# A decoder trunk's last gate: finished token block by token block, with the residual's scratch writes on ScalarE's queue

## The chip, the cores and the metric

The kernel runs on one core of one Trainium2 chip, as one launch. The metric is device time in microseconds (us), the median of repeated executions. The profile is a separate execution, taken by the hardware profiler; its time is given beside the others. TensorE (PE) does the matmuls, VectorE (DVE) and ScalarE (ACT) the elementwise work, GpSimd (POOL) some of it, and SyncE (SP) issues nearly all DMAs. Each engine works through its own queue in order.

## The reference, cut to what matters

A two-layer decoder trunk on 512 tokens of 1024 features, all in float32. The change is in the last two steps: the gated per-layer embedding of layer 1 and the final norm.

```python
def conv_ffn(xn, w_up, conv_w, conv_b, w_down):
    ...
    return (jax.nn.silu(g) * u) @ w_down

def per_layer_embed(h, p_i, g_norm, w_in, w_gate, b_gate):
    gate = jax.nn.sigmoid(rmsnorm(h, g_norm) @ w_gate + b_gate)
    return (p_i @ w_in) * gate

# reference(): for each layer
    h = h + conv_ffn(rmsnorm(h, norm_ffn[i]), ...)
    h = h + per_layer_embed(h, p[i], norm_ple[i], ple_w_in[i], ple_w_gate[i], ple_b_gate[i])
# at the end
    return rmsnorm(h, norm_final)
```

So the last gate needs the finished residual `h` of a token for its norm, then a 1024 x 1024 product, a sigmoid, a product with `p @ w_in`, an addition to `h`, and the mean square of the result for the final norm.

## The kernel before

**Numbers and layout.** Each float32 operand of a product is split into a high part (a cast to float32r) and a low part (the rest), and three matmuls are done for each block: high by high, low by high, high by low (`mm3`, `mm3t`). The residual lies with features on the partitions: eight tiles `h[0]` to `h[7]` of 128 features x 512 tokens. The products up to the last feed-forward keep that layout. The last gate turns it over: `mm3t` takes the normed residual as the stationary operand and the weights as the moving one, so its results have 128 tokens on the partitions and 512 features (a column half) along the row. There are four token blocks (`NC`) with two column halves each, eight feature blocks k in every product: 24 matmuls of 512 columns for a half. Because the gated result is in token layout, the old residual is needed in that layout too.

**Weights.** A planner lists all weights as units of at most 1024 columns. `load` brings a unit from HBM into one of six raw buffers (`RAWS`, tags r0 to r5), `pump_hi` lets ScalarE cast it to its high part (L187) and `pump` lets VectorE subtract for the low part (L196), into one of four pairs of buffers (`WBUFS`). The second column half of the last gate has buffers of its own: eight units of 512 columns in slots of the feed-forward's activations (`own`, `own_ah` and `own_al` in the profile). `chunk` hands a product its units and pumps a few units ahead. `load` is only called from `pump_hi` in this part of the kernel.

**The last down-projection.** `ffn(1, ...)` ends in `dense_add`: four chunks of 256 features, two blocks m each. For every block VectorE adds the product to `h[m]` (L383), then `norm.take(m)` makes the gate's scaled high and low operands (L280, L281) and the squares for its norm (L309, summed on GpSimd at L314, the last one on VectorE). Then `then(m)`, which is `turn_h(m)`: VectorE turns 32 x 32 blocks of `h[m]` into a tile `ht` (L965; tag c0, two buffers), and `write` sends the tile of the block before to a scratch array `rows` in HBM, four DMAs from SP (L959) of 64 KB each in runs of 128 bytes. The scratch array holds the residual in token layout; eight DMAs (L998) read it back into `hT`, in the order of the column halves.

**The last gate.** The first column half of all four token blocks runs with k = 0 to 5 first (72 matmuls), then k = 6 and 7 block by block; behind block 0's come eight small matmuls that sum the squares (`ms`, L990). From `ms` VectorE and GpSimd make the norm's root `np1rt` (L355, L357). Then, for each token block and half, `gated`: VectorE scales the product and adds the bias (`biased`, z, L1009), ScalarE takes the sigmoid (L1015), VectorE multiplies by the embedding and adds to `hT` (`summed`, L1016 and L1018); `square` sums the squares on ScalarE (L1028). The four first halves are gated together; then come the second halves of blocks 0 and 1, each with its final norm (`mean`, `root`, L1054), turned back (L1057) and written to `out` from SP (L1060); then block 2's second half and block 3's second half in two quarters. GpSimd multiplies the first halves of blocks 2 and 3 by the final gain ahead (L1044). Blocks 2 and 3 go out in token layout (`out_b`, L1078 and L1095).

**Order.** The framework orders the instructions of an engine by their place in the program and by when it reckons them ready, so one that is ready earlier can be moved ahead of its place. The last part (from `gate6` on) is held in the written order on VectorE, ScalarE and GpSimd by `in_order`; SP is not. SP's and ACT's DMAs signal their landing through a common set of semaphores.

Of the kernel before, what the change touches and what calls it, by code (L numbers as in the profile page):

```python
# [8 lines left out]
F32 = mybir.dt.float32  # L9
F32R = mybir.dt.float32r  # L10
U32 = mybir.dt.uint32
AF = mybir.ActivationFunctionType
ALU = mybir.AluOpType
# [39 lines left out]
def tile_yoco(ctx: ExitStack, tc: tile.TileContext, t, out: bass.AP, out_b: bass.AP):  # L53
# [12 lines left out]
    def psum(name, tag=None):  # L66
        if tag is None:
            tag = banks["tags"][banks["at"] % len(banks["tags"])]
            banks["at"] += 1
        return mmp.tile([P, S], F32, tag=tag, bufs=4 if tag == "mm" else 1, name=name)  # L70
# [135 lines left out]
    def chunk(cols, kk, ahead=WBUFS):  # L206

        pump(state["next"] + ahead)
        parts = []
        while len(parts) < kk:  # L210
            wh, wl, n = take()
            parts += [(wh, wl, j * cols) for j in range(n // cols)]
        assert len(parts) == kk
        return parts
# [11 lines left out]
    def mm3t(ps, xs, parts, c0, n, tok, first=True, last=True):  # L226

        for k, ((wh, wl, off), (xh, xl)) in enumerate(zip(parts, xs)):
            a, b = off + c0, off + c0 + n
            s = slice(tok * P, (tok + 1) * P)  # L230
            st = first and k == 0
            en = last and k == len(parts) - 1
            nc.tensor.matmul(ps, xh[:, s], wh[:, a:b], start=st, stop=False)
            nc.tensor.matmul(ps, xl[:, s], wh[:, a:b], start=False, stop=False)
            nc.tensor.matmul(ps, xh[:, s], wl[:, a:b], start=False, stop=en)
# [59 lines left out]
    class Norm:  # L295
# [11 lines left out]
        def square(self, k, eng=None):  # L307
            sq = tp.tile([P, S], F32, tag="sq", name=f"{self.name}sq{k}")
            nc.scalar.activation(sq, h[k], AF.Square)  # L309
            if self.acc is None:  # L310
                self.acc = sq
            else:
                acc = tp.tile([P, S], F32, tag="acc", name=f"{self.name}acc{k}")
                (eng or (nc.vector if k == KD - 1 else nc.gpsimd)).tensor_add(acc, self.acc, sq)  # L314
                self.acc = acc
# [50 lines left out]
    def dense_add(xs, kk, norm, fresh=False, then=None):  # L366

        for c in range(4):
            parts = chunk(256, kk)
            pss = []  # L370
            if fresh and c == 0:
                pss = [psum(f"d{j}") for j in range(2)]
                for k0, k1 in ((0, kk - 1), (kk - 1, kk)):
                    for j in range(2):
                        mm3(pss[j], parts[k0:k1], xs[k0:k1], j * P, first=k0 == 0, last=k1 == kk)
            for j in range(2):
                m = 2 * c + j
                if pss:
                    ps = pss[j]
                else:  # L380
                    ps = psum(f"d{m}")
                    mm3(ps, parts, xs, j * P)
                nc.vector.tensor_add(h[m], h[m], ps)  # L383
                if norm is not None:
                    norm.take(m)
                if then is not None:
                    then(m)

    def ffn(l, norm, nxt, then=None):
# [565 lines left out]
    def write(m, t):  # L955

        for q in range(P // SQ):
            c0 = m * P + q * SQ
            nc.sync.dma_start(rows[:, c0 : c0 + SQ].rearrange("(b i) j -> i b j", i=SQ),  # L959
                              t[q * SQ : (q + 1) * SQ, :].rearrange("p (b j) -> p b j", j=SQ))  # L960

    def turn_h(m):

        t = tp.tile([P, S], F32, tag="c0", name=f"ht{m}")
        nc.vector.transpose(t, h[m])  # L965
        if queue:
            write(*queue.pop())
        queue.append((m, t))
# [10 lines left out]
    hT = [hT[:2], hT[2:]]  # L979

    parts = chunk(S, KD)
    pss = [psum(f"gate{i}", "mm") for i in range(NC)]
    for i in range(NC):
        mm3t(pss[i], xs[:6], parts[:6], 0, S, i, last=False)
    ms = psum2("ms")[:, 0, :NC]
    for i in range(NC):
        mm3t(pss[i], xs[6:], parts[6:], 0, S, i, first=False)
        if i == 0:
            for j in range(NC):
                nc.tensor.matmul(ms[:, j : j + 1], npl.acc[:, j * P : (j + 1) * P], one, start=True, stop=True)  # L990
    rt = inv_root(ms, "np1", 1.0 / D)
    parts2 = chunk(S, KD, ahead=2 * WBUFS)
    for i in range(2):
        r = wp.tile([P, D], F32, tag=f"r{4 + i}", bufs=1, name=f"hT{2 + i}")
        hT.append([r[:, :S], r[:, S:]])
    for c in range(2):
        for i in range(NC):
            nc.sync.dma_start(hT[i][c], rows[i * P : (i + 1) * P, c * S : (c + 1) * S])  # L998

    ssq = const.tile([P, NC, 3], F32, name="ssq")  # L1000
    total = const.tile([P, NC], F32, name="total")
# [4 lines left out]
    def biased(i, c0, w, ps, n):  # L1006

        z = tp.tile([P, w], F32, tag="hs", name=f"z{i}_{n}")
        nc.vector.scalar_tensor_tensor(z, ps, rt[:, i : i + 1], brow[:, c0 : c0 + w], op0=ALU.mult, op1=ALU.add)  # L1009
        return z  # L1010
# [10 lines left out]
    def gated(i, c0, w, ps, n):  # L1021

        return summed(i, c0, w, biased(i, c0, w, ps, n), n)
# [6 lines left out]
    def mean(i, n, out_):  # L1030

        nc.vector.tensor_reduce(out_, ssq[:, i, :n], axis=mybir.AxisListType.X, op=ALU.add)  # L1032
        nc.vector.tensor_scalar(out_, out_, 1.0 / D, EPS, op0=ALU.mult, op1=ALU.add)  # L1033

    def root(i):

        r = rfin[:, i : i + 1]
        nc.gpsimd.tensor_tensor(r, total[:, i : i + 1], minus_half[:, :1], op=ALU.pow)
        return r

    for i in range(NC):
        square(i, gated(i, 0, S, pss[i], 0), 0)
    for i, dst in ((2, hT[2][0]), (end, yt[:, :S])):
        nc.gpsimd.tensor_mul(dst, hT[i][0], grow[:, :S])  # L1044

    flat = out.rearrange("k p s -> (k p) s")
    for i in range(2):
        ps = psum(f"gate{NC + i}", ("tr", "pv")[i])
        mm3t(ps, xs, parts2, 0, S, i)
        square(i, gated(i, S, S, ps, 1), 1)  # L1050
        mean(i, 2, total[:, i : i + 1])
        r = root(i)
        for c in range(2):
            nc.vector.scalar_tensor_tensor(hT[i][c], hT[i][c], r, grow[:, c * S : (c + 1) * S],  # L1054
                                           op0=ALU.mult, op1=ALU.mult)
            t = tp.tile([P, S], F32, tag=f"c{c}", name=f"y{i}_{c}")
            nc.vector.transpose(t, hT[i][c])  # L1057
            for q in range(P // SQ):
                s0 = i * P + q * SQ
                nc.sync.dma_start(flat[c * S : (c + 1) * S, s0 : s0 + SQ].rearrange("(f c) a -> c f a", c=SQ),  # L1060
                                  t[q * SQ : (q + 1) * SQ, :].rearrange("p (f a) -> p f a", a=SQ))

    others = const.tile([P, 1], F32, name="others")
    with in_order(*engines[1:]):
        ps = psum("gate6", "mm")
        mm3t(ps, xs, parts2, 0, S, 2)
        square(2, gated(2, S, S, ps, 1), 1)
        ps = psum("gate7", "mm")[:, :N]
        mm3t(ps, xs, parts2, 0, N, end)
        z = biased(end, S, N, ps, 1)  # L1070
        mean(2, 2, total[:, 2:3])
        r = root(2)
        hm = summed(end, S, N, z, 1)
        square(end, hm, 1)
        nc.scalar.activation(hT[2][0], hT[2][0], AF.Copy, scale=r)
        nc.vector.scalar_tensor_tensor(hT[2][1], hT[2][1], r, grow[:, S:], op0=ALU.mult, op1=ALU.mult)
        for c in range(2):
            nc.sync.dma_start(out_b[0, :, c * S : (c + 1) * S], hT[2][c])  # L1078
        nc.gpsimd.tensor_mul(yt[:, S : S + N], hm, grow[:, S : S + N])  # L1079
        mean(end, 2, others)  # L1080
        ps = psum("gate8", "mm")[:, :N]
        mm3t(ps, xs, parts2, N, N, end)
        hm = gated(end, S + N, N, ps, 2)
        sq = tp.tile([P, N], F32, tag="sq", name="sq_last")
        nc.vector.tensor_tensor_reduce(out=sq, in0=hm, in1=hm, scale=1.0 / D, scalar=others, op0=ALU.mult,
                                       op1=ALU.add, accum_out=total[:, end : end + 1])
        r = root(end)
        nc.vector.tensor_mul(yt[:, S + N :], hm, grow[:, S + N :])
        for q, (c0, c1) in enumerate(((0, 384), (384, D))):
            y = yt[:, c0:c1]  # L1090
            if q:
                nc.vector.tensor_scalar_mul(y, y, r)
            else:
                nc.scalar.activation(y, y, AF.Copy, scale=r)  # L1094
            (nc.sync if q else nc.scalar).dma_start(out_b[1, :, c0:c1], y)  # L1095
# [66 lines left out]
```

## Time and profile before

| | us |
|---|---|
| median of 3 runs | 1140.29 (1139.99 to 1140.67) |
| profiled execution | 1139.72 |
| its span, first to last instruction | 1138.0 |
| PE busy | 1120.3 (98%) |
| DVE busy | 735.6 (65%) |
| ACT busy | 506.4 (44%) |
| POOL busy | 137.7 (12%) |
| last matmul ends | 1123.0 of the span |

Times on the span are in microseconds from its first instruction. A timeline row has the start, the duration, the engine ("SPq" and "ACTq" are queues that issue DMAs), the line of the kernel, the operation, what is written and read, and in brackets how long the engine had been idle and what ended that. A row that merges several instructions ("x8") gives the time from the start of the first to the end of the last. A row of the windows gives, for each engine, the busy time and the number of instructions that started, then the granted clock, the share of the DMA engines' time and the rate.

### The profile page before, as it was taken

What the parts mean: (1) busy time and instruction counts of PE and PEld (TensorE: products, weight loads), DVE (VectorE), ACT (ScalarE), POOL (GpSimd) and SP (SyncE); (2) the same over time, 40 slices, a digit from 0 to 9 for tenths busy, and PEclk for the clock granted to TensorE, in tenths of its full rate; (3) what the DMA queues carried; (4) which work ended last, traced back from release to release, by engine and by line L of the source; (5) the groups of instructions that cost most, each with busy time, mean ns of one, the idle gap of its engine ahead of it and who ended that gap; (6) DMA issues with size and microseconds to landing.
All of it is one profiled execution on the core that took longest, in us unless ns stands there. A gap on an engine that the chain in (4) does not pass through costs nothing. (4 is left out here: it accounts for less than half of the span.)

```text
span 1138.0 us, 13493 instructions
## 1 busy us (share of the span) xinstructions
PE 1120.3 (98%) x5116; PEld 930.4 (82%) x5116; DVE 735.6 (65%) x973; ACT 506.4 (44%) x802; POOL 137.7 (12%) x161
## 2 busy tenths in 40 slices
PE   9999999999999999999999999999999999999994
PEld 7888888888888888888898887888888888888874
DVE  7356467763677367557868786677635774577656
ACT  6533344441344244445646776544313442344442
POOL 2100210000000000022225564200000000000212
PEclk9999999999999999999999999999999999999998
DMA  9322323323223323332054325333332333233263
GB/s 316 119 92 77 108 82 104 111 83 103 97 80 102 111 94 101 102 109 84 31 148 121 93 84 186 130 111 93 93 111 76 101 88 106 93 98 96 48 185 75
DMA packets 70097, 120.66 MB, mean 106 GB/s; under 512 B 30344, under 2 KB 41104, under 8 KB 70032
## 3 DMA queue, kind: packets, MB, share of 16 engines
q1 hardware_dynamic: 69600, 119.34, 33.9%
q8 instruction: 40, 0.66, 0.2%
q10 hardware_dynamic: 432, 0.46, 0.1%
q14 instruction: 25, 0.20, 0.1%
HBM read 110.33 MB, written 4.20 MB: 101 GB/s over the span
## 5 line engine op out<-in xcount | busy, mean ns | idle before, releaser
L196 DVE TENSOR_TENSOR wl<-wraw,wh 128x1024 fp32r<-128x1024 f32 (+2 forms) x197 | 238.9, 1214 | 121.0 <-ACT wh L187 120.3
L187 ACT CAST wh<-wraw 128x1024 fp32r<-128x1024 f32 (+1 forms) x196 | 202.0, 1032 | 244.4 <-PE d L223 134.8
L222 PE MATMUL up<-nf00h,wh 128*128 128x512 f32 x352 | 137.1, 389 | 0.0
L222 PE MATMUL up<-nf10h,wh 128*128 128x512 f32 x352 | 137.0, 389 | 0.0
L224 PE MATMUL up<-nf00h,wl 128*128 128x512 f32 x352 | 136.9, 389 | 0.0
L223 PE MATMUL up<-nf00l,wh 128*128 128x512 f32 x352 | 136.9, 389 | 0.0
L224 PE MATMUL up<-nf10h,wl 128*128 128x512 f32 x352 | 136.9, 389 | 0.0
L222 PE MATMUL d<-ah,wh 128*128 128x512 f32 x352 | 136.9, 389 | 0.0
L223 PE MATMUL d<-al,wh 128*128 128x512 f32 x352 | 136.9, 389 | 0.0
L224 PE MATMUL d<-ah,wl 128*128 128x512 f32 x352 | 136.9, 389 | 0.0
L223 PE MATMUL up<-nf10l,wh 128*128 128x512 f32 x352 | 136.9, 389 | 0.0
L411 ACT ACTIVATE c<-hs,vec 128x512 f32<-128x512 f32 x88 | 71.8, 815 | 89.0 <-DVE hs L407 87.9
L412 DVE SCALAR_TENSOR_TENSOR c<-hs,vec,c 128x511 f32<-128x511 f32 x88 | 65.9, 749 | 37.4 <-ACT c L411 37.2
L383 DVE TENSOR_TENSOR h<-h,d 128x512 f32<-128x512 f32 x56 | 38.4, 685 | 68.2 <-PE d L224 68.2
L284 ACT CAST ah<-a 128x512 fp32r<-128x512 f32 x44 | 27.4, 622 | 113.5 <-DVE a L417 113.5
L222 PEld LDWEIGHTS up<-nf00h,wh 128*128 128x128 f32 x352 | 66.1, 188 | 13.8
L223 PEld LDWEIGHTS up<-nf10l,wh 128*128 128x128 f32 x352 | 66.1, 188 | 13.8
L222 PEld LDWEIGHTS d<-ah,wh 128*128 128x128 f32 x352 | 66.1, 188 | 13.8
L224 PEld LDWEIGHTS up<-nf10h,wl 128*128 128x128 f32 x352 | 66.1, 188 | 13.8
L223 PEld LDWEIGHTS d<-al,wh 128*128 128x128 f32 x352 | 66.1, 188 | 13.7
L224 PEld LDWEIGHTS d<-ah,wl 128*128 128x128 f32 x352 | 66.1, 188 | 13.7
L224 PEld LDWEIGHTS up<-nf00h,wl 128*128 128x128 f32 x352 | 66.1, 188 | 13.7
(292 smaller groups left out, 1978.9 us busy)
## 6 DMA issues: line engine op xcount, KB each, us to landing
wraw<-in_w_up SPq DMA_DIRECT2D x88, 512.0 KB, 3.5
wraw<-in_w_down SPq DMA_DIRECT2D x32, 512.0 KB, 3.5
wraw<-in_w_down SPq DMA_DIRECT2D x16, 384.0 KB, 3.2
wraw<-in_w_u SPq DMA_DIRECT2D x8, 512.0 KB, 7.3
wraw<-in_w_out SPq DMA_DIRECT2D x8, 512.0 KB, 3.5
wraw<-in_w_gate SPq DMA_DIRECT2D x8, 512.0 KB, 4.2
wraw<-in_w_q SPq DMA_DIRECT2D x8, 512.0 KB, 3.5
wraw<-in_w_o SPq DMA_DIRECT2D x8, 512.0 KB, 3.2
```

Source lines behind the costliest of these rows:

```text
L187: nc.scalar.copy(wh[:, :n], src)
L196: nc.vector.tensor_sub(wl[:, :n], src, wh[:, :n].bitcast(F32))
L222: nc.tensor.matmul(ps, wh[:, a:b], xh, start=st, stop=False)
L223: nc.tensor.matmul(ps, wh[:, a:b], xl, start=False, stop=False)
L224: nc.tensor.matmul(ps, wl[:, a:b], xh, start=False, stop=en)
L284: nc.scalar.copy(hi, src)
L383: nc.vector.tensor_add(h[m], h[m], ps)
L411: nc.scalar.activation(c, hs, AF.Identity, bias=v("conv_b", l * 2 * NJ + col), scale=cw[2])
L412: nc.vector.scalar_tensor_tensor(c[:, 1:], hs[:, : S - 1], cw[1], c[:, 1:], op0=ALU.mult, op1=ALU.add)
```

## The change

Four things are changed, all at the end of the kernel:

- The 32 writes of the residual to `rows` are issued from ScalarE's queue, not SP's, and the turned tiles alternate between the tags c0 and c1, so four buffers, not two.
- In the last down-projection, ahead of every `then(m)`, raw weights are loaded up to six units past the last one pumped.
- The last gate starts with the first halves of token blocks 0 and 1 alone (k = 0 to 5, then 6 and 7 with `ms` behind block 0's). The units of the second half are pumped between these two steps. The reads of `hT` stand there too and go by token block. Then the second halves of blocks 0 and 1 follow, each with its final norm and output; both halves of block 2 in a row with its final norm and output; the first half of block 3 and its two quarters.
- Block 2's final scaling is done by VectorE for both halves, with the gain in the same instruction; the GpSimd multiplication for block 2 goes, that for block 3's first half stays.

```diff
@@ dense_add @@
                 if then is not None:
+                    load(state["unit"] + RAWS)
                     then(m)
@@ write, turn_h @@
-            nc.sync.dma_start(rows[:, c0 : c0 + SQ].rearrange("(b i) j -> i b j", i=SQ),
+            nc.scalar.dma_start(rows[:, c0 : c0 + SQ].rearrange("(b i) j -> i b j", i=SQ),
...
-        t = tp.tile([P, S], F32, tag="c0", name=f"ht{m}")
+        t = tp.tile([P, S], F32, tag=f"c{m % 2}", name=f"ht{m}")
@@ last gate @@
-    pss = [psum(f"gate{i}", "mm") for i in range(NC)]
+    pss = [psum(f"gate{i}", "mm") for i in range(2)]
+    for i in range(2):
+        mm3t(pss[i], xs[:6], parts[:6], 0, S, i, last=False)
+    parts2 = chunk(S, KD)
...
     for i in range(NC):
-        mm3t(pss[i], xs[:6], parts[:6], 0, S, i, last=False)
+        for c in range(2):
+            nc.sync.dma_start(hT[i][c], rows[i * P : (i + 1) * P, c * S : (c + 1) * S])
     ms = psum2("ms")[:, 0, :NC]
-    for i in range(NC):
+    for i in range(2):
         mm3t(pss[i], xs[6:], parts[6:], 0, S, i, first=False)
...
-    parts2 = chunk(S, KD, ahead=2 * WBUFS)
...
-    for i in range(NC):
-        square(i, gated(i, 0, S, pss[i], 0), 0)
-    for i, dst in ((2, hT[2][0]), (end, yt[:, :S])):
-        nc.gpsimd.tensor_mul(dst, hT[i][0], grow[:, :S])
...
+    def half(i, c):
+
+        if c == 0 and i < 2:
+            ps = pss[i]
+        else:
+            ps = psum(f"gate{i}_{c}")
+            mm3t(ps, xs, parts2 if c else parts, 0, S, i)
+        square(i, gated(i, c * S, S, ps, c), c)
+
+    def finish(i):
+
         mean(i, 2, total[:, i : i + 1])
         r = root(i)
         for c in range(2):
             nc.vector.scalar_tensor_tensor(hT[i][c], hT[i][c], r, grow[:, c * S : (c + 1) * S],
                                            op0=ALU.mult, op1=ALU.mult)
+            if i == 2:
+                nc.sync.dma_start(out_b[0, :, c * S : (c + 1) * S], hT[i][c])
+                continue
...
+    for i in range(2):
+        half(i, 0)
+    for i in range(2):
+        half(i, 1)
+        finish(i)
+    for c in range(2):
+        half(2, c)
+    finish(2)
+    half(end, 0)
+    nc.gpsimd.tensor_mul(yt[:, :S], hT[end][0], grow[:, :S])
...
     with in_order(*engines[1:]):
-        ps = psum("gate6", "mm")
-        mm3t(ps, xs, parts2, 0, S, 2)
-        square(2, gated(2, S, S, ps, 1), 1)
         ps = psum("gate7", "mm")[:, :N]
         mm3t(ps, xs, parts2, 0, N, end)
-        z = biased(end, S, N, ps, 1)
-        mean(2, 2, total[:, 2:3])
-        r = root(2)
-        hm = summed(end, S, N, z, 1)
+        hm = gated(end, S, N, ps, 1)
         square(end, hm, 1)
-        nc.scalar.activation(hT[2][0], hT[2][0], AF.Copy, scale=r)
-        nc.vector.scalar_tensor_tensor(hT[2][1], hT[2][1], r, grow[:, S:], op0=ALU.mult, op1=ALU.mult)
-        for c in range(2):
-            nc.sync.dma_start(out_b[0, :, c * S : (c + 1) * S], hT[2][c])
```

More of the change, by code (lines that the diff above doesn't have):

```diff
@@ L981, in tile_yoco @@
     parts = chunk(S, KD)
-    pss = [psum(f"gate{i}", "mm") for i in range(NC)]
+    pss = [psum(f"gate{i}", "mm") for i in range(2)]
[3 more added lines that the diff above has]
+    for i in range(2):
+        r = wp.tile([P, D], F32, tag=f"r{4 + i}", bufs=1, name=f"hT{2 + i}")
+        hT.append([r[:, :S], r[:, S:]])
     for i in range(NC):
-        mm3t(pss[i], xs[:6], parts[:6], 0, S, i, last=False)
+        for c in range(2):
+            nc.sync.dma_start(hT[i][c], rows[i * P : (i + 1) * P, c * S : (c + 1) * S])
     ms = psum2("ms")[:, 0, :NC]
-    for i in range(NC):
+    for i in range(2):
         mm3t(pss[i], xs[6:], parts[6:], 0, S, i, first=False)
@@ L991, in tile_yoco @@
     rt = inv_root(ms, "np1", 1.0 / D)
-    parts2 = chunk(S, KD, ahead=2 * WBUFS)
-    for i in range(2):
-        r = wp.tile([P, D], F32, tag=f"r{4 + i}", bufs=1, name=f"hT{2 + i}")
-        hT.append([r[:, :S], r[:, S:]])
-    for c in range(2):
-        for i in range(NC):
-            nc.sync.dma_start(hT[i][c], rows[i * P : (i + 1) * P, c * S : (c + 1) * S])
     ssq = const.tile([P, NC, 3], F32, name="ssq")
@@ L1039, in root @@
         return r
-    for i in range(NC):
-        square(i, gated(i, 0, S, pss[i], 0), 0)
-    for i, dst in ((2, hT[2][0]), (end, yt[:, :S])):
-        nc.gpsimd.tensor_mul(dst, hT[i][0], grow[:, :S])
     flat = out.rearrange("k p s -> (k p) s")
[L1047 to L1050, printed above, removed]
+    def half(i, c):
[6 more added lines that the diff above has]
+    def finish(i):
         mean(i, 2, total[:, i : i + 1])
@@ L1061, in tile_yoco @@
                                   t[q * SQ : (q + 1) * SQ, :].rearrange("p (f a) -> p f a", a=SQ))
+    for i in range(2):
+        half(i, 0)
+    for i in range(2):
+        half(i, 1)
[5 more added lines that the diff above has]
+    nc.gpsimd.tensor_mul(yt[:, :S], hT[end][0], grow[:, :S])
     others = const.tile([P, 1], F32, name="others")
     with in_order(*engines[1:]):
-        ps = psum("gate6", "mm")
-        mm3t(ps, xs, parts2, 0, S, 2)
-        square(2, gated(2, S, S, ps, 1), 1)
         ps = psum("gate7", "mm")[:, :N]
         mm3t(ps, xs, parts2, 0, N, end)
-        z = biased(end, S, N, ps, 1)
-        mean(2, 2, total[:, 2:3])
-        r = root(2)
-        hm = summed(end, S, N, z, 1)
+        hm = gated(end, S, N, ps, 1)
         square(end, hm, 1)
-        nc.scalar.activation(hT[2][0], hT[2][0], AF.Copy, scale=r)
-        nc.vector.scalar_tensor_tensor(hT[2][1], hT[2][1], r, grow[:, S:], op0=ALU.mult, op1=ALU.mult)
-        for c in range(2):
-            nc.sync.dma_start(out_b[0, :, c * S : (c + 1) * S], hT[2][c])
         nc.gpsimd.tensor_mul(yt[:, S : S + N], hm, grow[:, S : S + N])
```

## The prediction

> **What bounds the kernel now.** I read the page's first block, then the windows of the last 70 us, then the waits and timelines of single engines there.
>
> ```profile
> span 1138.0 us, 13493 instructions
> PE 1120.3 (98%) x5116; PEld 930.4 (82%) x5116; DVE 735.6 (65%) x973; ACT 506.4 (44%) x802; POOL 137.7 (12%) x161
> ```
>
> PE is busy throughout, so two things can be won: the stalls of PE, and the time from its last matmul to the end. The windows give, for each stretch, the busy time of PE, PEld, DVE, ACT and POOL, the clock, the DMA share and GB/s:
>
> ```profile
> 1047.00:1057.00 10.00, 10.00 (x45) 8.26 (x44) 8.25 (x11) 5.42 (x8) 2.60 (x2) 1.00 0.49 107
> 1067.00:1077.00 10.00, 10.00 (x46) 8.28 (x45) 6.30 (x8) 4.50 (x6) 3.08 (x2) 1.00 0.27 46
> 1085.00:1094.00 9.00, 9.00 (x46) 7.55 (x44) 0.00 (x0) 2.67 (x4) 0.00 (x0) 1.00 0.82 226
> 1094.00:1108.00 14.00, 13.15 (x59) 10.61 (x59) 13.47 (x22) 8.19 (x15) 1.97 (x1) 1.00 0.65 208
> 1123.00:1138.00 15.00, 0.00 (x1) 0.00 (x0) 7.58 (x20) 3.18 (x8) 2.60 (x3) 0.64 0.39 105
> ```
>
> VectorE does nothing from 1085 to 1094, is full from 1094 to 1108, and 15.0 us pass after the last matmul. So the end is set by work that began late on VectorE. Why it idled, from the timelines of PE, DVE and POOL:
>
> ```profile
> 1080.35 0.39 PE L233 MATMUL gate<-wh,np10h 128*128 128x512 f32 x1
> 1081.03 0.39 PE L233 MATMUL gate<-wh,np10h 128*128 128x512 f32 x1
> 1093.28 0.95 PE L990 MATMUL ms<-one,np1acc 128*128 128x1 f32 x8
> 1095.65 0.50 PE L235 MATMUL gate<-wl,np10h 128*128 128x512 f32 x1 [0.85 <-DVE wl L196]
> 1122.61 0.28 PE L234 MATMUL gate<-own_ah,np10l 128*128 128x256 f32 x1
> 1122.72 0.28 PE L235 MATMUL gate<-own_al,np10h 128*128 128x256 f32 x1
> 1094.27 0.16 DVE L355 TENSOR_SCALAR np1m<-ms 128x4 f32<-128x4 f32 x1 [10.41 <-PE ms L990]
> 1094.51 1.97 POOL L357 TENSOR_TENSOR np1rt<-np1m,minus_half 128x4 f32<-128x4 f32 x1 [18.70 <-DVE np1m L355]
> 1097.33 0.74 DVE L1009 SCALAR_TENSOR_TENSOR z<-gate,np1rt,row_m 128x512 f32<-128x512 f32 x1
> 1128.46 0.47 DVE L1009 SCALAR_TENSOR_TENSOR z<-gate,np1rt,row_m 128x256 f32<-128x256 f32 x1
> ```
>
> Three matmuls take 0.68 us, so a half (24) takes 5.44. The norm's sums stand behind 78 matmuls, the first z comes at 1097.3, and the last z starts 5.46 us after PE ends at 1123.0. And SP's queue:
>
> ```profile
> 1049.93 35.88 SPq L959 DMA_DIRECT2D rows<-ht  x32
> 1085.91 12.42 SPq L164 DMA_DIRECT2D wraw<-in_w_gate  x18
> 1134.20 0.35 SPq L1078 DMA_DIRECT2D out<-hT  x1
> 1134.65 0.38 SPq L1095 DMA_DIRECT2D out<-yt  x1
> SPq L1078 <- DMA out<-yt: 5.0, 1, 5.0
> ACT wh L187 <- DMA wraw<-in_w_gate: 11.1, 1, 11.1
> ```
>
> The gate's last weights are only issued once the scratch writes are out: ScalarE waits 11.1 us for them, and PE the 0.85 above. At the end, block 2's second output waits on SP for the landing of ACT's `out<-yt`, and the last output stands behind it.
>
> **The change part by part.** *Start of the gate.* PE's work is the same: 7 halves of 5.44, the sums, two quarters of 24 matmuls at 0.12 (last two rows: 1122.61, 1122.72), together 38.1 + 0.8 + 5.8 = 44.7 us. From the first matmul at 1077.0 it ends at 1121.9 with the last one's latency, 1.0 before now, if PE doesn't stall. The sums now stand behind 42 matmuls: 1077.0 + 9.5 + 0.8 = 1087.3; root (0.16 + 1.97) at 1089.6. So z can start near 1090, 7 us earlier, and falls into the time in which VectorE idles.
>
> *VectorE behind PE.* From then on a half arrives every 5.44 us. What VectorE needs for one, from token block 1's second half:
>
> ```profile
> 1116.91 0.71 DVE L1009 SCALAR_TENSOR_TENSOR z<-gate,np1rt,row_m 128x512 f32<-128x512 f32 x1
> 1119.04 0.69 DVE L1018 TENSOR_TENSOR hT<-hT,gs 128x512 f32<-128x512 f32 x1
> 1121.59 1.42 DVE L1054 SCALAR_TENSOR_TENSOR hT<-hT,rfin,row_m 128x512 f32<-128x512 f32 x2 [0.67 <-POOL rfin L1038]
> 1122.93 1.30 DVE L1057 STREAM_TRANSPOSE y<-hT 128x512 f32<-128x512 f32 x2
> ```
>
> Round trips to ScalarE and GpSimd included: 2.8 us to the addition, 6.1 to the scaled row, 7.3 to the turned one. If VectorE takes each half to its end before it starts the next, with PE's first second half done at 1094.4: 7.3 + 7.3 (blocks 0, 1), 2.8 + 6.1 (block 2; the scaling that ScalarE did is in it), 2.8 (block 3), 2.7 for the first quarter (1.8, as the last quarter's z to its addition below, and 0.9 of square and mean) = 29.0, so 1123.4 for the last z. PE is done at 1121.9. Any overlap between halves brings it toward 1122.0. I take 1123.4, the serial value, because the queues are in order and the program finishes a block before it goes on. Now it is 1128.46: a gain of 5.1.
>
> One contention is moved: block 3's GpSimd product now runs beside the first quarter.
>
> ```profile
> 1107.68 0.69 DVE L1016 TENSOR_TENSOR gs<-gs,pet 128x512 f32<-128x512 f32 x1
> 1109.13 1.67 DVE L1016 TENSOR_TENSOR gs<-gs,pet 128x512 f32<-128x512 f32 x1
> 1108.66 1.59 POOL L1044 TENSOR_TENSOR hT<-hT,row_m 128x512 f32<-128x512 f32 x1 [12.18 <-ACT sq L1028]
> ```
>
> The same product takes 1.67 instead of 0.69 beside GpSimd: up to 1.0 us on the path, at most once, since GpSimd needs 1.6. I count nothing, as the serial value is already the upper one, and keep the 1.0 for the range. [...]
>
> *The end.* From the last z:
>
> ```profile
> 1129.88 0.42 DVE L1018 TENSOR_TENSOR hT<-hT,gs 128x256 f32<-128x256 f32 x1
> 1131.60 0.55 DVE L1092 TENSOR_SCALAR yt<-yt,rfin 128x640 f32<-128x640 f32 x1 [0.44 <-POOL rfin L1038]
> out<-yt SPq DMA_DIRECT2D x1, 320.0 KB, 2.4
> out<-yt ACTq DMA_DIRECT2D x1, 192.0 KB, 1.9
> ```
>
> Scaled at 1132.15, but issued at 1134.65: 2.5 us of waiting. Block 2's outputs now leave five matmul groups earlier, near 1117, so this wait goes; SP's output queue is empty by then. z to scaled is unchanged (3.7), landing 2.4, and 0.9 from landing (1134.65 + 2.41) to 1138.0. New span: 1123.4 + 3.7 + 2.4 + 0.9 = 1130.4, rounded with the issue gap to 1130.5. Against 1138.0 that is -7.5: 1.0 of PE, 4.1 of lag, 2.4 at the end (what comes late next is PE itself). The profiled execution took 1139.72, 1.7 over its span, so 1132.2; the median of the runs is 0.57 above it: **1132.8**.
>
> *What the gain must be paid with: ScalarE's queue.*
>
> ```profile
> L959 SPq DMA_DIRECT2D rows<-ht x32: 303/490/1152, 1049.9 to 1085.3; - x32
> 1074.88 1.05 ACT L187 CAST wh<-wraw 128x1024 fp32r<-128x1024 f32 x1 [0.52 <-PE d L223]
> 1079.06 0.62 ACT L309 ACTIVATE np1sq<-h 128x512 f32<-128x512 f32 x1
> L187 ACT CAST own_ah<-wraw 128x512 fp32r<-128x512 f32 x8 | 4.8, 617 | 2.1 <-DMA wraw<-in_w_gate 2.1
> 1101.30 0.62 ACT L187 CAST own_ah<-wraw 128x512 fp32r<-128x512 f32 x1 [0.70 <-DMA wraw<-in_w_gate]
> wraw<-in_w_up SPq DMA_DIRECT2D x88, 512.0 KB, 3.5
> ```
>
> 32 issues at 0.49 are 15.7 us, in which ScalarE computes nothing; I price an ACT issue like SP's. Two feature blocks take PE 9.5 us, ScalarE about 4.5 to 5.4 (windows) and now 3.9 more: 8.4 to 9.3. It fits, hidden by its idle time, barely. Queued behind a write are the casts of the coming weights and the gate's operands; PE waits for those. The tightest is the gate's third unit: cast until 1075.9, its low part by 1077.2 (reckoned at a little over the cast's own 1.05), needed by PE at 1077.0 + 12 x 0.227 = 1079.7: a margin of 2.5 us against one block's writes, 4 x 0.49. The last block's operands and squares (done at 1079.7 on ScalarE) are needed at 1077.0 + 36 x 0.227 = 1085.1. From 1077 on, two casts (2.1), the last two blocks' writes (3.9), the last operands and squares (two instructions like the 0.62 one) and eight own casts (4.8) end near 1089.1; PE needs the own units one by one from 1088.6 to 1093.4. The load edit costs SP issue time only, and a raw buffer that is refilled early has been cast already. The two more `ht` buffers let VectorE turn the last block without its wait. I count zero, with 3 us of PE stall as the other bound.
>
> The writes themselves: the windows show a DMA share of 0.27 to 0.49 while they go, so it is the queue, not the engines, that holds the weights back. [...]
>
> **Rivals.** *1, part of it given back:* ScalarE falls behind a little, and PE stalls 2 to 4 us at the gate's third unit or at the own units. Everything behind shifts: 1134.8 to 1137, near 1136. For it: 8.4 to 9.3 of 9.5 us. Against: margins of 2.5 to 5.
>
> *2, slower:* SP's waiting 5.0 us for a DMA of ACT shows that the two queues' DMAs are coupled. If ScalarE's writes likewise have to wait for the landing of a prefetched load, ScalarE stands still, casts and all. One landing per block (3.5 us, the median for weights, last row above) makes 8 x 3.5 + 15.7 = 44 us. Of the 38 us between 1047 and 1085 it is busy some 18, at the windows' rates, and idle 20, so it would come 24 late; less 5 of margin PE ends 19 later, less the gain of 7.5: 1152. It is slower than before from 2.5 + 7.5 = 10 us of lateness. Against it: writes are four per block and 4.8 us apart, longer than a load's landing.
>
> *3, only the end:* VectorE's lag stays, because halves are finished out of step with PE; then only 1.0 and 2.4 are won: 1136.9.
>
> *4, no effect:* the loads stay late in spite of the edit. If the own units come as now, with the last cast at 1101.3 (row above), PE reaches the first second half's end at 1103 instead of 1094 and ends 9 later: 7.5 less 9, about 1141.
>
> **How the numbers follow.** About 0.2% (2.3 us) is what a measurement can tell from no change. Chances: forecast 0.62, rival 1 0.16, rival 3 0.06, rival 4 0.06, rival 2 0.10. The low end is the forecast without lag: z at 1122.0, 1.4 less, and 0.5 for an output that lands in 1.9, as ACT's does: 1130.9, taken as 1130.8. The high end takes in rivals 1 and 3 with the 1.0 of contention: 1137.9. Faster 0.83 (forecast, 3 and nearly all of 1), same 0.06, slower 0.11.
>
> **What would show it.** The gate's matmuls without an idle gap over 1 us until about 1122; first z near 1090; last z within 2 us of PE's end; the final `out<-yt` issued within 0.1 us of its scaling; ScalarE's writes with gaps, not solid, and no wait of a cast for a `rows<-ht` landing. Wrong if PE idles for `wl` or `own` units after 1077, or if ACT's writes wait for `wraw` landings.

## The result, and the profile after

The changed kernel takes 1144.59 us (median of 7 runs, 1142.81 to 1144.88), the kernel before 1140.72 on the same chip (7 runs, 1139.99 to 1141.51): a ratio of the means of 1.0027, interval 1.0016 to 1.0039. It is slower by 0.3%, where 0.7% faster was forecast. The profiled execution took 1144.59 us, 1.7 over its span. The page's first block, and the windows (busy time of PE, PEld, DVE, ACT, POOL, then the granted clock, DMA share, GB/s), of the changed kernel:

```profile
span 1142.9 us, 13466 instructions
PE 1123.6 (98%) x5116; PEld 932.2 (82%) x5116; DVE 736.2 (64%) x974; ACT 505.4 (44%) x801; POOL 134.6 (12%) x160
...
1067.00:1077.00 10.00, 7.82 (x28) 6.00 (x27) 5.49 (x6) 1.96 (x3) 1.58 (x1) 0.83 0.39 110
1085.00:1094.00 9.00, 9.00 (x38) 7.40 (x36) 2.00 (x4) 2.05 (x3) 0.00 (x0) 0.83 0.54 118
1094.00:1108.00 14.00, 13.19 (x60) 10.66 (x60) 11.60 (x18) 7.74 (x14) 1.93 (x1) 1.00 0.61 187
1123.00:1138.00 15.00, 8.29 (x60) 7.66 (x58) 11.51 (x23) 5.10 (x13) 2.80 (x4) 0.93 0.27 66
```

Two rows are new: from 1067 to 1077 TensorE is idle for 2.2 us, and there and from 1085 to 1094 it runs at a granted clock of 0.83. Before, both stretches were full at 1.00. VectorE is still nearly idle from 1085 to 1094 (2.00 of 9), so the early z of the forecast did not come. The timelines of PE, DVE and ACT:

```profile
1067.83 0.39 PE L223 MATMUL d<-al,wh 128*128 128x512 f32 x1
1070.40 0.50 PE L224 MATMUL d<-ah,wl 128*128 128x512 f32 x1 [2.18 <-DVE wl L196]
1071.75 0.63 PE L222 MATMUL d<-ah,wh 128*128 128x512 f32 x1
1072.18 0.63 PE L223 MATMUL d<-al,wh 128*128 128x512 f32 x1
1081.20 0.39 PE L233 MATMUL gate<-wh,np10h 128*128 128x512 f32 x1
1083.99 0.50 PE L235 MATMUL gate<-wl,np10h 128*128 128x512 f32 x1 [2.18 <-DVE wl L196]
1131.01 0.28 PE L235 MATMUL gate<-own_al,np10h 128*128 128x256 f32 x1
1061.01 1.79 ACT L187 CAST wh<-wraw 128x1024 fp32r<-128x1024 f32 x2 [0.75 <-issue]
1067.81 0.69 DVE L383 TENSOR_TENSOR h<-h,d 128x512 f32<-128x512 f32 x1 [2.69 <-PE d L224]
1068.53 0.71 DVE L966 STREAM_TRANSPOSE ht<-h 128x512 f32<-128x512 f32 x1
1069.17 3.14 DVE L196 TENSOR_TENSOR wl<-wraw,wh 128x1024 fp32r<-128x1024 f32 x2
1078.00 0.71 DVE L281 SCALAR_TENSOR_TENSOR np10l<-h,vec,np10h 128x512 fp32r<-128x512 f32 x1
1081.40 0.69 DVE L383 TENSOR_TENSOR h<-h,d 128x512 f32<-128x512 f32 x1 [2.69 <-PE d L224]
1076.28 2.00 ACT L187 CAST wh<-wraw 128x1024 fp32r<-128x1024 f32 x2 [6.51 <-DMA rows<-ht]
1082.76 2.32 DVE L196 TENSOR_TENSOR wl<-wraw,wh 128x1024 fp32r<-128x1024 f32 x2
1091.95 1.99 ACT L187 CAST wh<-wraw 128x1024 fp32r<-128x1024 f32 x2 [8.59 <-DMA rows<-ht]
1094.43 0.16 DVE L355 TENSOR_SCALAR np1m<-ms 128x4 f32<-128x4 f32 x1 [7.43 <-PE ms L998]
1101.24 0.74 DVE L1010 SCALAR_TENSOR_TENSOR z<-gate,np1rt,row_m 128x512 f32<-128x512 f32 x1
1135.29 0.47 DVE L1010 SCALAR_TENSOR_TENSOR z<-gate,np1rt,row_m 128x256 f32<-128x256 f32 x1
```

Twice TensorE waits 2.18 us for VectorE's low parts (`wl`). At the first, ScalarE's casts were done at 1062.8; VectorE sat idle from 1065.1 to 1067.8, waiting for the product of an addition, and only behind that addition and its turn did it make the low parts (1069.17). The idle time would have held nearly all of them; they stood behind the addition in VectorE's queue. At the second, the gate's third matmul needs the low part of the gate's first unit. ScalarE's casts come late there, at 1076.28, behind writes that held its queue for 6.5 us, but they are done at 1078.28. VectorE is idle from 1078.71 to 1081.40, again until the product of an addition is there, and makes the low parts behind that addition and its turn, at 1082.76. The casts of the gate's third and fourth unit come at 1091.95, after 8.6 us behind writes. Up to the sums of the norm at 1093.4, TensorE does 36 matmuls with the first two units: a unit holds two feature blocks, six matmuls for each half, so these are the shares of three halves. Then it waits 0.8 us for the third unit's low part.

VectorE takes up the sums of the norm at 1094.43, the first z follows at 1101.24, and TensorE ends at 1131.29. Behind each of the two long stalls the matmuls start 0.43 us apart instead of 0.23, for 3.41 us by the trace's clock record: 8 matmuls that would have taken 1.8 us, so another 1.6 us lost each time.

The end is as forecast in kind (SP's and ACT's queues, and the last scaling):

```profile
1130.41 1.01 SPq L1061 DMA_DIRECT2D out<-hT  x2
1138.43 0.55 DVE L1100 TENSOR_SCALAR yt<-yt,rfin 128x640 f32<-128x640 f32 x1 [0.44 <-POOL rfin L1039]
1139.01 0.33 SPq L1103 DMA_DIRECT2D out<-yt  x1
1139.07 0.36 ACTq L1103 DMA_DIRECT2D out<-yt  x1
```

Scaled at 1138.98, issued at 1139.01: the wait of 2.5 us is gone. But the scaling itself comes 11.9 us later than forecast (1127.1).

### The profile page after: what moved, and what is told of

It is laid out like the page before. It is cut to its first block, busy times and chain, and to the rows that moved or that the text cites. A ratio compares the mean times of both kernels' runs of the same rounds, so it can differ in the third digit from the quotient of the medians.

```text
span 1142.9 us, 13466 instructions
## 1 busy us (share of the span) xinstructions
PE 1123.6 (98%) x5116; PEld 932.2 (82%) x5116; DVE 736.2 (64%) x974; ACT 505.4 (44%) x801; POOL 134.6 (12%) x160
## 4 chain that ended last, share of the span: by engine, by line
PE 93%; DVE 2%; DMA 1%; issue 1%; ACT 1%; ACTq 0%; SPq 0%; POOL 0%; POOLq 0%
PE up L222 14%; PE up L224 14%; PE up L223 14%; PE d L224 8%; PE d L223 8%; PE d L222 8%; PE o L222 1%; PE q L222 1%; PE o L223 1%; PE o L224 1%; PE sc L738 1%; PE q L224 1%; PE gate L222 1%; PE q L223 1%; PE u L222 1%
## 5 line engine op out<-in xcount | busy, mean ns | idle before, releaser
L223 PEld LDWEIGHTS up<-nf00l,wh 128*128 128x128 f32 x352 | 66.1, 188 | 13.7
```

Of the source, the lines that this page charges most:

```text
L223: nc.tensor.matmul(ps, wh[:, a:b], xl, start=False, stop=False)
```

## The experiments

Fourteen kernels, called by the first part of their names below. The theories, as the expectations name them. A: ScalarE's queue is the cause. B: the early loads are. C: the order by token blocks is. D, formed after the first set: the framework, which is free to move instructions within an engine, put them in a bad order; the mechanism of the forecast is right where the order is held. E: the writes themselves cost ScalarE its time, whatever the order. Times are medians; ratios are to the kernel before on the same chip, of the means, with their 95% intervals. The kernel before took 1140.3 to 1140.6 us on the three chips of these runs.

**First set: one part of the change undone, or done alone.**

`e1_sp_writes`, the change with its writes back on SP:

```diff
-            nc.scalar.dma_start(rows[:, c0 : c0 + SQ]...
+            nc.sync.dma_start(rows[:, c0 : c0 + SQ]...
```

> The changed kernel with one part undone: the residual's scratch writes go back to SP's queue; the four tile buffers, the early loads and the order by token blocks stay. Theory A (ScalarE's queue: the 32 writes stand ahead of the weights' casts, and VectorE's low parts are ordered behind the additions that wait for PE): both PE stalls of 2.2 us (at 1068 and 1082) go, the gate starts at 1077, first z near 1090, last z within 2 us of PE's end, 1131 to 1135 us. Theory B (the early loads are at fault: they take raw buffers and landing semaphores, which whoever issues the writes has to wait for): the stalls stay, or SP holds the loads back; 1141 to 1145 us. Theory C (the order by token blocks itself starves PE): at least one stall stays, 1141 us or more.

Measured: 1147.52 us, ratio 1.0066 (1.0051 to 1.0081). TensorE has no gap and ends at 1121.69 (forecast of the prediction: 1121.9), the first z starts at 1088.57 (forecast: near 1090). Yet the time is worse than with the writes on ScalarE. VectorE's timeline:

```profile
1094.85 0.69 DVE L1019 TENSOR_TENSOR hT<-hT,gs 128x512 f32<-128x512 f32 x1
1113.34 0.75 DVE L1010 SCALAR_TENSOR_TENSOR z<-gate,np1rt,row_m 128x512 f32<-128x512 f32 x1 [17.80 <-PE gate L235]
```

TensorE worked on pieces of several halves and finished none: from 1095.5 to 1113.3 VectorE has nothing to take, then everything at once, and the last z starts at 1135.07, 13.4 us behind the last matmul. A is right about the stalls and wrong about the total; C has the total, 1141 or more, but not its stall.

`e2_act_only`, the kernel before with only the writes moved to ScalarE (the edit of e1 in reverse, on the kernel before):

> The kernel before with one part alone: the scratch writes on ScalarE's queue; two tile buffers, no early loads, old order. Theory A: PE stalls of about 2 us in the last down-projection and at the gate's start, each with some 1.7 us of half clock behind it, 4 to 8 us over the kernel before: 1144 to 1149 us. Theory B: without the early loads there is nothing to wait for, 1139.5 to 1141.5 us. Theory C: no change either, 1139.5 to 1141.5 us.

Measured: 1142.25 us, 1.0019 (1.0009 to 1.0029), outside all ranges. The stalls are there, 1.47 us and 1.46 us; the mean granted clock of the profiled execution is 0.995, as in the kernel before. TensorE's waits (us in total, times, longest):

```profile
PE gate L235 <- DVE wl L196: 2.3, 2, 1.5
PE d L224 <- DVE wl L196: 1.5, 1, 1.5
```

`e3_no_load`, the change without its early loads (`load(state["unit"] + RAWS)` taken out):

> The changed kernel without the early loads; writes on ScalarE's queue, four tile buffers, order by token blocks. Theory A: the stalls stay, and the own units come later still: 1142 to 1149 us. Theory B: the stalls go, 1131 to 1137 us. Theory C: stalls stay, 1142 to 1149 us.

Measured: 1143.69 us, 1.0030 (1.0018 to 1.0042), with the same two stalls of 2.18 us, as A and C said. B falls.

`e4_blocks_only`, the kernel before with only the new last gate (its order by token blocks and block 2's scaling on VectorE):

> The kernel before with the order by token blocks alone: writes on SP, two tile buffers, no early loads. Theory A: no stall in the down-projection; the own units are issued behind the writes, as before, so PE waits for them at the first second half, 3 to 6 us with the half clock; the final wait of SP goes; 1136 to 1141 us. Theory B: like A. Theory C: 1143 us or more, PE stalls already at the gate's first units.

Measured: 1142.32 us, 1.0019 (1.0009 to 1.0028), between the ranges of A and C. One wait of 4.7 us on TensorE; the mean granted clock of the profiled execution is 0.993, where the kernel before has 0.995. SP's queue shows why TensorE waited:

```profile
PE gate L233 <- ACT wh L187: 4.7, 1, 4.7
1050.36 39.02 SPq L959 DMA_DIRECT2D rows<-ht  x32
1089.48 9.86 SPq L164 DMA_DIRECT2D wraw<-in_w_gate  x18
```

The wait comes behind 54 matmuls of the gate, the shares of three halves in its first three units: it is the fourth unit that is missing, and its load still stands behind the writes. No single part carries the loss, and no part undone brings the gain.

**Second set: the order held.** `in_order` is the kernel's own helper, which makes each instruction of an engine follow the one before it in the program. `e7_pe_order` is e1 with TensorE held through the gate:

```diff
+    with in_order(engines[0]):
         for i in range(2):
             mm3t(pss[i], xs[:6], parts[:6], 0, S, i, last=False)
...
-    with in_order(*engines[1:]):
+    with in_order(*engines):
         ps = psum("gate7", "mm")[:, :N]
```

> The first of these kernels with the writes back on SyncE's queue (1147.5 us), and TensorE held in the written order through the gate: block 0's and 1's first halves, then one half after the other. Theory D (what fails is the order in which the framework put the instructions; the forecast's own mechanism is right): no gap on TensorE above 1 us, its end at 1121 to 1123, first z near 1089, no z after 1125, VectorE's lag behind the last matmul 1.5 to 3 us, 1131 to 1135 us. Rival (TensorE's order does not matter, the 17.8 us in which VectorE waited only fill time that the end needs anyway): the last z stays later than 1130 and the time is 1143 or more.

Measured: 1134.71 us, 0.9948 (0.9933 to 0.9963): 12.8 us better than e1 by the order of TensorE's matmuls alone. TensorE ends at 1123.61 and the last z starts at 1125.43, 0.6 and 0.4 later than D expected; the lag is 1.8.

`e8_act_pe_order`, the changed kernel (writes on ScalarE) with the same two edits:

> The changed kernel with its writes left on ScalarE's queue, and only TensorE held in the written order through the gate. Theory D: the two stalls of 2.2 us ahead of the gate stay, with 3.4 us of half clock behind each, so TensorE ends near 1131 as in the changed kernel; the lag of the last z goes from 4.0 to 1.5 to 3 us: 1142 to 1144 us. Rival (the queue costs only where TensorE's order is wrong): the gate ends by 1125 and the time is under 1138 us.

Measured: 1147.43 us, 1.0060 (1.0043 to 1.0077): outside both ranges. Its waits on TensorE:

```profile
PE gate L233 <- ACT wh L187: 3.5, 1, 3.5
PE gate L235 <- DVE wl L196: 2.2, 1, 2.2
PE d L224 <- DVE wl L196: 2.2, 1, 2.2
```

The two stalls stay, as D said, but a third joins: behind twelve matmuls of the gate, at its third unit. Held in order, TensorE cannot run ahead with other halves while it waits for the late casts. Its lag is not better either (last z 1.8 behind a last matmul at 1137.05). So holding TensorE pays only where its weights come in time.

`e9_act_all_order`, e8 with VectorE and ScalarE held through the last down-projection too:

```diff
     def dense_add(xs, kk, norm, fresh=False, then=None):
+        with in_order(*(engines[1:3] if then is not None else ())):
             for c in range(4):
```

> The changed kernel with its writes left on ScalarE's queue; TensorE held in the written order through the gate, and VectorE and ScalarE held in the written order through the last down projection (each pair of weight casts and low parts stands directly behind the second addition of the quarter before). Theory D: the stalls of 2.2 us shrink under 1 us, no half clock, TensorE ends at 1121 to 1125, the time is 1131 to 1136 us. Rival E (the writes themselves hold ScalarE's queue: 32 issues of some 0.4 us and their waits for landings): stalls of 1.4 us or more and a gate that begins after 1079 us stay, 1139 us or more.

Measured: 1134.76 us, 0.9950 (0.9936 to 0.9965), with ScalarE's and TensorE's waits:

```profile
ACT own_ah L187 <- DMA rows<-ht: 5.6, 1, 5.6
PE gate L235 <- DVE own_al L196: 0.8, 1, 0.8
```

ScalarE still waits 5.6 us behind writes; but the casts that TensorE needs next now stand ahead of them. TensorE ends at 1124.04.

`e10_act_down_order`, e9 with TensorE's order in the gate left free:

> As the kernel before it, but with TensorE's order in the gate left to the framework. Theory D: no stall of 2 us and no half clock, TensorE ends at 1121 to 1125; but it takes a second half or the end of a first half late, and VectorE's lag behind the last matmul is 4 us or more: 1135 to 1146 us, at least 2 us above the kernel before it. Rival E: the stalls stay as in the changed kernel, 1142 us or more, and both kernels are within 1 us of each other where the order matters nothing.

Measured: 1142.07 us, 1.0013 (1.0004 to 1.0023), 7.3 us above e9. TensorE ends at 1123.32 with no stall above 0.43 us, but the last z starts at 1131.18. VectorE's waits:

```profile
DVE z L1011 <- PE gate L235: 10.7, 2, 10.0
```

So the loss has two parts that hide each other: 1144.59 with neither order held, 1147.43 with TensorE's alone, 1142.07 with the others alone, 1134.76 with both.

**Third set: which order, and what the queue itself costs.** `e11_act_order` is e2 with VectorE and ScalarE held as in e9:

> The kernel before with its scratch writes on ScalarE's queue (1142.25 us when the framework was free to choose the order) and VectorE and ScalarE held in the written order through the last down projection; nothing else of the change. Theory D (the writes cost only by the order that the framework then chose): no gap of TensorE above 1 us ahead of the gate, the gate starts by 1078, 1139 to 1141 us, within 1 us of its control, the same order with the writes on SyncE's queue. Rival E (ScalarE pays for the writes themselves, and the better time with the order held came from elsewhere): 1142 us or more, 1.5 us or more above the control.

Measured: 1140.96 us, 1.0006 (0.9997 to 1.0015). TensorE has no gap at all and ends at 1121.93, 1.1 earlier than before; the stalls of e2 were order. The end swallows the gain: the last scaling is at 1131.0, but SP issues the last output at 1135.63.

`e12_before_order`, meant as its control, writes on SP:

> Control: the kernel before with VectorE and ScalarE held in the written order through the last down projection, the writes on SyncE's queue. Theory D: the kernel before had these casts in step already, so the order by itself moves nothing: 1139 to 1141.5 us. Rival (the held order is a gain of its own, and the good times of the kernels that have it say nothing of the change): 1137 us or less.

Measured: 1149.18 us, 1.0078 (1.0066 to 1.0091). It missed all ranges, and as a control it failed: TensorE waited 9.36 us. Its wait and SP's queue:

```profile
PE gate L233 <- ACT wh L187: 9.4, 1, 9.4
1051.39 40.88 SPq L960 DMA_DIRECT2D rows<-ht  x32
1092.37 11.76 SPq L164 DMA_DIRECT2D wraw<-in_w_gate  x20
```

The held order put VectorE's last turn behind an operation that waits for TensorE, the last four writes behind that, and the gate's weights from its third unit on behind them on SP. In this order and without the early loads, SP's queue is the worse place for the writes, by 8.2 us; with the order left free it was the better one, by 1.9 (the kernel before and e2).

`e14_dve_down_order`, e9 with only VectorE held through the down-projection (`engines[1:2]`):

> The changed kernel, writes on ScalarE's queue, TensorE held in the written order through the gate, and of the last down projection only VectorE held (ScalarE's order left to the framework). Theory D in its narrow form (the low parts of VectorE that stood behind two additions were the stall): no gap of 2 us, 1134 to 1137 us. Rival (ScalarE's casts behind the writes, which wait up to 8.6 us for landings, are the stall, and VectorE's low parts only follow them): gaps of 1.4 us or more stay, 1139 us or more.

Measured: 1140.58 us, 0.9998 (0.9990 to 1.0007). Both stalls of 2.18 us are gone, with the writes still on ScalarE's queue. One of 4.38 us is left, at the gate's thirteenth matmul, which needs its third unit, as in e8. TensorE's wait and ScalarE there:

```profile
PE gate L233 <- ACT wh L187: 4.4, 1, 4.4
1079.05 3.84 ACTq L961 DMA_DIRECT2D rows<-ht  x6
1082.93 1.99 ACT L187 CAST wh<-wraw 128x1024 fp32r<-128x1024 f32 x2 [3.53 <-DMA rows<-ht]
```

So VectorE's order made the two stalls, as the narrow form of D says. D's time is missed all the same: the casts of the third and fourth unit stand behind six writes, and that is ScalarE's share.

`e17_act_cast_order`, the other way round, only ScalarE held (`engines[2:3]`):

> The changed kernel, writes on ScalarE's queue, TensorE held in the written order through the gate, and of the last down projection only ScalarE held (VectorE's order left to the framework, which again puts the low parts behind two additions). Theory D, each stall by its own engine: the first stall near 1068 is VectorE's and stays at 2.2 us with its 3.4 us of half clock, and as ScalarE is late by what VectorE gives it, the second stays too: 1143 to 1148 us. Rival (ScalarE's order alone is the cause of both): no gap of 1.4 us, 1134 to 1137 us.

Measured: 1148.33 us, 1.0068 (1.0055 to 1.0080), 0.3 us above D's range, with stalls of 1.01, 2.18, 2.18 and 3.54 us. With VectorE's order free both stalls of 2.18 stay, and holding ScalarE's alone helps nothing.

`e18_sp_all_order`, the clean control: e9 with its writes on SP (early loads kept):

> Clean control to the kernel with all orders held and writes on ScalarE's queue (1134.76 us): the same early loads, blocks and held orders, the writes on SyncE's queue. Theory D (the writes cost nothing on ScalarE's queue once the order is held): 1133 to 1136 us, within 1.2 us of it. Rival E (the writes cost ScalarE 32 issues and their waits, 5.6 us of them seen as idle ahead of the casts): 2 us or more below it, 1132.8 or less. Against both: if the weight loads stand behind SyncE's writes again, TensorE waits more than 1.4 us for a load and the time is over 1138 us.

Measured: 1134.85 us (1134.45 to 1135.28), 0.9950 (0.9936 to 0.9964), beside e9's 1134.76 (1134.52 to 1135.49). With loads early and orders held, the queue of the writes costs nothing and gains nothing. E falls.

**The better version.** `e16_casts` is e7 with ScalarE's casts of the gate's last units ahead of its first sigmoid, and two of their low parts ahead of VectorE's mean:

```diff
+        casts = in_order(engines[2])
+        casts.__enter__()
+        traced = nc.cur_bb.bb.instructions
+        n0 = len(traced)
         parts2 = chunk(S, KD)
+        lows = [i for i in traced[n0:] if i.engine == engines[1]]
...
+        n0 = len(traced)
         rt = inv_root(ms, "np1", 1.0 / D)
+        first = next(i for i in traced[n0:] if i.engine == engines[1])
+        tc.add_manual_dep(first, lows[3].name, ...
...
             half(i, 0)
+            if i == 0:
+                casts.__exit__(None, None, None)
```

> A better version: writes on SyncE's queue, TensorE held in the written order through the gate (1134.7 us), and now ScalarE's casts of the gate's last eight weight units held ahead of its first sigmoid, the low parts of the third and fourth ahead of VectorE's mean. Theory D: the last gaps of TensorE in the gate (0.72 us together) go, TensorE ends at 1122.0 to 1123.2, 1133.4 to 1134.6 us. Rival (VectorE's chain sets the end, not TensorE): 1134.5 to 1135.5 us.

Measured: 1132.74 us (1132.66 to 1132.98), 0.9932 (0.9919 to 0.9946), below the range of D: 7.9 us faster than the kernel before, 11.9 faster than the changed one. Its first and last z, last matmul, last scaling and last output:

```profile
1089.06 1.41 DVE L1020 SCALAR_TENSOR_TENSOR z<-gate,np1rt,row_m 128x512 f32<-128x512 f32 x2 [1.14 <-POOL np1rt L357]
1121.88 0.28 PE L235 MATMUL gate<-own_al,np10h 128*128 128x256 f32 x1
1123.48 0.48 DVE L1020 SCALAR_TENSOR_TENSOR z<-gate,np1rt,row_m 128x256 f32<-128x256 f32 x1
1126.63 0.55 DVE L1112 TENSOR_SCALAR yt<-yt,rfin 128x640 f32<-128x640 f32 x1 [0.44 <-POOL rfin L1049]
1127.21 0.33 SPq L1115 DMA_DIRECT2D out<-yt  x1
```

TensorE has no gap from 1047 on.

## Why the prediction was wrong

| us of the span | forecast | changed | e9 | e16 |
|---|---|---|---|---|
| first z | 1090 | 1101.2 | 1089.5 | 1089.1 |
| TensorE ends | 1121.9 | 1131.3 | 1124.0 | 1122.2 |
| last z | 1123.4 | 1135.3 | 1126.4 | 1123.5 |
| scaled | 1127.1 | 1139.0 | 1130.0 | 1127.2 |
| span | 1130.5 | 1142.9 | 1133.7 | 1131.1 |

The span missed by 12.4: 9.4 in TensorE's end, 2.5 in the lag behind it (4.0 instead of 1.5), 0.5 at the end.

*The step that failed* first is "I count zero, with 3 us of PE stall as the other bound", under ScalarE's queue. It took the casts and low parts at the places they have in the trace of before and asked whether ScalarE has the time. It has: e9 and e18 are equal. The 15.7 us "in which ScalarE computes nothing" were an estimate; in the trace of the changed kernel the write issued at 1064.12 took 0.50 us, beside the activations of 1063.77 (0.72 us) and 1064.40 (0.62). But the change altered the order in which the framework put VectorE's and ScalarE's instructions. The stalls (2 x 2.18 and 0.8 at 1095), with 1.6 of half clock behind each of the long ones, make 8.4 of the 9.4; the rest stays open. "The tightest is the gate's third unit" named the wrong place. The first stall lies ahead of the gate, where no margin was reckoned, and the second is at the gate's first unit: its low part was made at 1066.45 before and only at 1082.76 now. The third unit did lose its margin of 2.5, for its cast begins at 1091.95 instead of 1074.88; but TensorE had other matmuls until then. Where its order is held and it cannot run ahead, it waits there for 3.5 to 4.4 us (e8, e14, e17). The two stalls go with VectorE's order alone (e14), this wait only with ScalarE's as well (e9).

The trace of before had a sign of it, which the prediction misread. It put TensorE's 0.85 us there down to the late loads. But the cast in question was done at 1091.78. The low part was made at 1094.38, directly behind the first instruction for the norm's root (1094.27), for which VectorE had waited idle for 10.4 us. It was VectorE's order there too:

```profile
1090.73 1.05 ACT L187 CAST wh<-wraw 128x1024 fp32r<-128x1024 f32 x1 [11.06 <-DMA wraw<-in_w_gate]
1094.38 1.22 DVE L196 TENSOR_TENSOR wl<-wraw,wh 128x1024 fp32r<-128x1024 f32 x1
```

*The other step that failed* is "the program finishes a block before it goes on". TensorE is not held in the gate. In e1, where nothing stalls, that alone costs 12.8 us (e7). In the changed kernel the first second half's z comes at 1107.64 instead of about 1094.4. TensorE takes up that half's weights (`own`) only at 1100.90, 11.9 later than reckoned (1094.4 less the 5.44 of a half). Of this, 8.8 us are the lateness that it already has (the gate begins at 1081.2 instead of 1077.0; then come 2.2, 0.8 and 1.6 of half clock), and 2.7 are twelve matmuls of a third half that it does first: 60 with `wh` ahead of the first with `own`, where e9 has 48. That half's weights are late as well: SP issues the last eight DMAs of their loads only at 1095.75, and the last low part is made at 1103.28. Whether this alone would have held TensorE, no run shows.

```profile
1083.97 1.94 SPq L164 DMA_DIRECT2D wraw<-in_w_gate  x4
1095.75 3.84 SPq L164 DMA_DIRECT2D wraw<-in_w_gate  x8
```

*What was right.* VectorE's serial price: from that z to the last one 29.0 was forecast, 27.65 measured (1107.64 to 1135.29). The end: 2.4 forecast; the last output is issued 0.03 us behind its scaling. TensorE's 1.0, where it does not stall: 1.3 in e1, 0.8 in e16. The load edit at nothing: e3. That e16 lands at 1132.74 beside the forecast of 1132.8 is partly chance, for there the first second half comes 1.9 later than reckoned (1096.3) and the chain from it is 1.8 shorter (27.2); but each step is within 2 us of its forecast. The contention with GpSimd, counted at nothing and kept at 1.0 for the range, came in the changed kernel: beside GpSimd (1132.86, 1.26 us) an addition of 128x256 took 1.39 us at 1133.01, where the one at 1129.88 of the kernel before took 0.42.

*The rivals.* Rival 1 had the kind, stalls of 2 to 4 us, but not the place, and it left out the half clock and the lag. Rival 2's coupling exists: ScalarE's writes go out at 1057.82, 1074.72 and 1075.39, each 0.02 us behind the landing of a weight load of SP, and its casts wait 15.1 us behind writes:

```profile
ACT wh L187 <- DMA rows<-ht: 15.1, 2, 8.6
```

Its price of 44 us was far too high, and e9 pays nothing for it. Both signs that the prediction named for being wrong were seen. The chance of 0.11 for slower was too small: it was given to one mishap, while a framework that reorders can make several. Rival 4's sum gives 1141.8 (1132.8 and 9), not 1141.

Not settled: why the framework chose these orders. No run holds TensorE in the old order of the gate, so how much of the 6.2 us between e11 and e9 is the rest of the change, and how much the hold, stays open. The changed kernel's runs lie at two levels, three at 1142.8 with a mean granted clock of 0.995 and four at 1144.6 to 1144.9 with 0.994. One stretch of half clock more or less (3.41 us, 0.0015 of the span's clock, 1.6 us) would fit; there is no trace of the faster level.

## What to carry to other kernels

Where a framework orders instructions, a change of one queue or one block order moves the places of others; so a forecast from the old trace can fail for the new program, as here, unless the order is pinned. Before pricing an engine's spare time, ask what stands ahead of the instruction that the bottleneck needs next: the same writes on ScalarE gave 1147.4 us in e8 and 1134.8 in e9. Undoing one part is not enough where two losses hide each other: pin TensorE's order and its feeders' order separately and together.

## What the runs showed of the hardware

In the changed kernel a stall of TensorE cost nearly twice its length. After each of the two gaps of 2.18 us (matmuls again from 1070.40 and 1083.99) the clock record has 3.41 us at a granted clock of 0.5, from 1071.05 and from 1084.71, so 2.18 us of waiting cost some 3.8. Shorter gaps show none of it: 0.85 us in the kernel before and 0.8 in the changed kernel (at 1095) and in e9 lie in windows with a granted clock of 1.00. In e8, with gaps of 2.2, 2.2 and 3.5 us, the windows from 1067 to 1108 have clocks of 0.83, 0.96, 0.69 and 0.86. Taken as stretches at 1.0 and at 0.5, the two values in the changed kernel's record, that makes 13.5 us at half clock; less twice 3.41, some 6.7 stand behind the gap of 3.5. This last figure is an estimate. How long a gap must be to bring half clock was not shown.

What the queue of the writes cost depended on what stood behind them: 0.1 us between e9 and e18, 8.2 between e11 and e12, and 1.9 the other way between the kernel before and e2. In the second pair the issue of the weights was held up: e12's SP issued 20 DMAs of the gate's weights only from 1092.37 on, behind writes that took its queue 40.88 us.
